# The adds of the modulation sums on VectorE instead of GpSimd, and one modulation block moved to a later stage

## The chip, the cores and the metric

One Trainium2 chip, one of its cores. The metric is the device time of one execution in microseconds, the median of several runs. The kernel computes two transformer blocks in one launch; this text is about a stretch of about 450 us in the first third of it.

## The reference, cut to what matters

Every layer is modulated by rows that come from the conditioning vector `c`: a vector-matrix product with a weight of 1024 x 6144, split into six parts. Here is what the change touches: layer 0's dense feed-forward, and the modulation of layer 1 and of its shared keys and values.

```python
c_act = jax.nn.silu(c)
for layer in range(DEPTH):
    mod = c_act @ w_ada[layer] + b_ada[layer]
    a_shift, a_scale, a_gate, f_shift, f_scale, f_gate = jnp.split(mod, 6, axis=-1)
    if layer == N_A_LAYERS:
        kc, vc, k_slc, v_slc, k_win, v_win = nsa_shared_kv(h, c_act, kv_gain, w_kv_ada, b_kv_ada, ...)
    u = modulate(rmsnorm(h, attn_gain[layer]), a_shift, a_scale)
    ...

def modulate(u, shift, scale):
    return u * (1.0 + scale[:, None, :]) + shift[:, None, :]

def swiglu(u, wg, wu, wd):
    return (jax.nn.silu(u @ wg) * (u @ wu)) @ wd
```

There are 256 tokens, a width of 1024, and a hidden width of 2816 in the dense layer.

## The kernel before, in words

**Stages.** `run` goes through layer 0's attention, its dense feed-forward (`ffn0`, about 190 to 431 us of the trace), layer 1's projections and attention (`layer1`, `layer1_out`, about 431 to 656 us), and then a mixture of experts, a second mixer and a second mixture. Weights come from HBM in chunks of 128 x 2048 f32 (1 MB), all issued in one order on SyncE's queue (SP). The instructions of each engine are put in an order by a scheduler when the program is built; on the chip every engine, and SP with its transfers, takes them strictly in that order.

**The dense stage.** 11 steps, each with three 1 MB chunks: gate (`ffg`), up (`ffu`), down (`ffd`). Products are made exact enough by splitting a weight into a high and a low part: ScalarE copies `raw` to `wh` (L425), VectorE subtracts to get `wl` (L426), and TensorE multiplies three times. `gu` are the gate and up products (48 matmuls each, L454, L455, L457), `ffacc` the down products (24 matmuls a step, L462 to L464), one step behind. Between them ScalarE applies silu (`hid`, L936), VectorE multiplies (L937) and splits the result into `hh` and `hl` (L425, L426). There are four `raw` buffers, three `wh`, three `wl`.

**Modulation blocks.** A block is 1024 x 2048 of a modulation weight, 8 chunks of 1 MB. There are two ways to compute one. `ada_block` (L479 to L493, called by `ada`) streams the chunks through two `adaw` buffers into TensorE: 4 matmuls a chunk, in four column groups of the array (L491), 32 in a block; then `ada_columns` copies the sums (`adaacc`, L502), brings them into columns with 4 small matmuls (L506) and adds the bias (L509). `ada_sums` (L511 to L532) is for stages in which TensorE is busy: ScalarE scales each chunk by its values of `c` (L523), GpSimd adds it to a running sum `adasum` (L525, 7 adds a block), and TensorE sums only over the partitions at the end (4 matmuls, L529). It is a generator: each `next(sums)` in `ffn0` records one chunk. It has four `adaw` buffers and two `adasum` buffers; a buffer's next load waits for the add that reads it.

**Who uses what.** `ffn0` computes four blocks this way: "k" 0 (for the shared keys and values), and "1" 0, 1 and 2 (all of layer 1's). Block "1" 2 holds layer 1's f_scale and f_gate, columns 32 to 47 of `mod1`; they are read by `moe_ahead` in `layer1_out`, behind the attention, and later. `ada("2", 0)` and `ada("2", 1)` are blocks of the second mixer's modulation, computed the direct way in and around layer 1.

Of the kernel before, what the change touches and what calls it, by code (L numbers as in the profile page):

```python
# [14 lines left out]
ALU = mybir.AluOpType  # L15
# [220 lines left out]
class Build:  # L236
# [274 lines left out]
    def ada_sums(self, blocks):  # L511


        nc = self.nc
        for n, b in blocks:
            total = self.act.tile([P, 2048], F32, tag="adasum", name=self.name("adasum"), bufs=2)
            for k in range(8):
                w = total
                if k:
                    pool, bufs = (self.act, 2) if k % 2 else (self.adap, self.ada_bufs)  # L520
                    w = pool.tile([P, 2048], F32, tag="adaw", name=self.name("adaw"), bufs=bufs)
                nc.sync.dma_start(w[:], self.A["ada" + n][b][:, k * 2048:(k + 1) * 2048])
                nc.scalar.activation(w[:], w[:], AF.Identity, scale=self.c_col[:, k:k + 1])  # L523
                if k:
                    nc.gpsimd.tensor_tensor(total[:], total[:], w[:], op=ALU.add)  # L525
                yield
            acc = self.pc([P, 512], name="ada")
            for g in range(4):
                nc.tensor.matmul(acc[32 * g:32 * g + 32, :], self.ones[:, :32], total[:, g * 512:(g + 1) * 512], start=True,  # L529
                                 stop=True, tile_position=(0, 32 * g))  # L530
            s = slice(16 * b, 16 * b + 16)
            self.ada_columns(acc, [({"0": self.mod0, "1": self.mod1, "k": self.modk}[n][:, s], self.sm("b_ada" + n)[:, s])])  # L532
# [371 lines left out]
    def ffn0(self):  # L904
        nc, A = self.nc, self.A
        r = self.rstd(self.h)
        g = self.gain1(self.sm("fg0"), self.mod0[:, 32:40], "fg0")
        u, = self.norm_T(self.h, r, [(g, self.mod0[:, 24:32])])
        acc = [self.pa([P, 2, 512], name="ffacc%d" % m) for m in range(2)]
        pend = []  # L910
        sums = self.ada_sums([("k", 0), ("1", 0), ("1", 1), ("1", 2)])

        def down():
            hid, w, j = pend.pop(0)
            wh, wl = self.split(w)
            for f in range(2):
                for m in range(2):
                    for n in range(2):
                        a = tuple(x[:, f, m * P:(m + 1) * P] for x in hid)
                        b = tuple(x[:, f, n * 512:(n + 1) * 512] for x in (wh, wl))  # L920
                        self.mm3(acc[m][:, n, :], a, b, start=j + f == 0, stop=j + f == 11)

        for j in range(11):
            wgu = [self.load(A[n][j], (8, 256))[0] for n in ("ffg", "ffu")]
            wd = self.load(A["ffd"][j], (2, 1024))[0]
            pg = []
            for i in range(2):
                wh, wl = self.split(wgu[i])
                ps = self.pb([P, 2, 256], name="gu")
                for ff in range(2):  # L930
                    s = slice(ff * P, (ff + 1) * P)
                    self.products_T(ps[:, ff, :], wh[:, :, s], wl[:, :, s], u)
                pg.append(ps)
                next(sums, None)
            hid = self.tl("s2", (2, 256), name="hid")
            nc.scalar.activation(hid, pg[0][:], AF.Silu)  # L936
            nc.vector.tensor_tensor(hid, hid, pg[1][:], op=ALU.mult)  # L937
            hh = self.tl("s2", (2, 256), F32R, name="hh")
            hl = self.tl("s2", (2, 256), F32R, name="hl")
            self.split_to(hh, hl, hid)  # L940
            if j:
                down()
                next(sums, None)
            pend.append(((hh, hl), wd, j))
        self.whole(sums)
        down()
        gate = self.tl("s4", (1024,), name="gate")
        for i in range(2):
            ps = self.pb([P, 4, P])
            for k in range(4):  # L950
                nc.tensor.matmul(ps[:, k, :], self.mod0[:, 40 + 4 * i + k:41 + 4 * i + k].to_broadcast([P, P]), self.ident,
                                 start=True, stop=True)
            nc.scalar.activation(gate[:, i * 512:(i + 1) * 512], ps[:].rearrange("p a b -> p (a b)"), AF.Copy)
        for m in range(2):
            tmp = self.tl("s4", (1024,), name="res")
            nc.vector.tensor_tensor(tmp, acc[m][:].rearrange("p a b -> p (a b)"), gate, op=ALU.mult)
            nc.vector.tensor_tensor(self.h[:, m, :], self.h[:, m, :], tmp, op=ALU.add)
# [137 lines left out]
    def layer1_out(self, qT, br, extra):  # L1095
        A = self.A
        oh = self.tl("s8", (8, 256), F32R, name="oh")
        ol = self.tl("s8", (8, 256), F32R, name="ol")
        self.ada("2", 0)
        with self.banks("att1", 0, 0):  # L1100
            self.attend(qT, br, oh, ol, extra)
        self.ada("2", 1)
        with self.banks("out1", 2, 3):
            gate = self.bcast_row(self.mod1[:, 16:24])
            t = self.moe_ahead(self.sm("rt1"), self.sm("fg1"), self.mod1[:, 32:40], self.mod1[:, 24:32])
            for b in range(2):
                self.residual(self.dense_tok((oh, ol), A["b_out"][b], 512, apart=True), b, gate)
                if b == 0:
                    for m in range(2):
                        self.squares(self.h, self.ss1, m, 0)  # L1110
        return t
# [1226 lines left out]
```

## Time and profile before

| what | us |
|---|---|
| median of 3 runs | 2009.3 (2007.61 to 2012.69) |
| the profiled execution, its own time | 2009.72 |
| its span in the trace | 2007.9 |
| TensorE busy in the span | 1827.2 (91%) |
| VectorE busy | 1013.6 (50%) |
| ScalarE busy | 771.9 (38%) |
| GpSimd busy | 222.0 (11%) |

Between the span and the time of the same execution lie 1.8 us. The busy time of an instruction runs from its start to its end. The granted clock is TensorE's, as a share of 2.4 GHz; it has two levels, and a stretch's value is the mean over them. Idle times in square brackets stand before an instruction and name what ended them.

### The profile page before, as it was taken

How to read it: one execution, taken by the hardware profiler on the slowest of the kernel's cores; microseconds unless marked ns; L12 is line 12 of the kernel's file. 1: busy time of each engine (PE TensorE's matmuls, PEld its weight loads, DVE VectorE, ACT ScalarE, POOL GpSimd, SP SyncE). 2: the span in 40 equal slices, each digit the busy share in tenths (PEclk: the TensorE clock that was granted, in tenths of full speed). 3: DMA queues.
4: the chain of work that ended last, by engine and by line, in shares of the span. 5: the costliest groups of instructions: out<-in, count | busy, mean ns of one | idle time of the engine just before them, and what ended most of it. 6: DMA issues, size and time to landing. Idle time of an engine off the chain costs nothing. (4 is left out here: it accounts for less than half of the span.)

```text
span 2007.9 us, 25685 instructions
## 1 busy us (share of the span) xinstructions
PE 1827.2 (91%) x9658; PEld 1174.9 (59%) x9658; DVE 1013.6 (50%) x1382; ACT 771.9 (38%) x961; POOL 222.0 (11%) x128
## 2 busy tenths in 40 slices
PE   4998799979999799999999999998999699899996
PEld 2656698856756685455555555554554486535452
DVE  3775787775554673344434534444542566524234
ACT  3355556632364463342333333433331453212131
POOL 0100856621000200000000200000000200100000
PEclk8999899989899899999999999999999899899998
DMA  8783577954611699999999999999999425599995
GB/s 338 266 310 147 214 285 299 355 230 155 261 71 51 232 346 384 422 403 376 405 422 402 380 410 377 422 414 402 346 422 421 183 87 208 190 405 354 409 420 214
DMA packets 128947, 624.29 MB, mean 311 GB/s; under 512 B 14512, under 2 KB 14768, under 8 KB 90800
## 3 DMA queue, kind: packets, MB, share of 16 engines
q1 hardware_dynamic: 127552, 619.59, 78.4%
q10 hardware_dynamic: 1264, 2.98, 0.4%
q8 instruction: 79, 1.29, 0.2%
q14 instruction: 52, 0.43, 0.1%
HBM read 621.46 MB, written 1.05 MB: 310 GB/s over the span
## 5 line engine op out<-in xcount | busy, mean ns | idle before, releaser
L426 DVE TENSOR_TENSOR wl<-raw,wh 128x2048 fp32r<-128x2048 f32 (+1 forms) x207 | 526.9, 2554 | 353.5 <-ACT wh L425 308.0
L425 ACT ACTIVATE wh<-raw 128x2048 fp32r<-128x2048 f32 (+1 forms) x207 | 391.4, 1899 | 275.3 <-DMA raw<-in_moe 142.3
L1428 PE MATMUL gu<-raw,xT 128*64 128x512 f32 (+2 forms) x1600 | 353.0, 592 | 9.2 <-DMA raw<-in_moe 9.0
L1428 PEld LDWEIGHTS gu<-raw,xT 128*64 128x64 f32 (+1 forms) x1600 | 102.9, 132 | 206.9 <-issue 162.5
L1428 PE MATMUL down<-raw,hh 128*64 128x512 f32 (+1 forms) x784 | 169.0, 598 | 0.6 <-DMA raw<-in_moe 0.6
L525 POOL TENSOR_TENSOR adasum<-adasum,adaw 128x2048 f32<-128x2048 f32 x28 | 151.5, 5414 | 67.8 <-ACT adaw L523 59.9
L1419 PE MATMUL gu<-wh,xT 128*128 128x512 f32 x368 | 148.6, 404 | 2.1 <-ACT wh L425 2.1
L1420 PE MATMUL gu<-wh,xT 128*128 128x512 f32 x368 | 144.7, 393 | 0.0
L1428 PEld LDWEIGHTS down<-raw,hh 128*64 128x64 f32 (+1 forms) x784 | 49.3, 132 | 90.0 <-issue 78.5
L1422 PE MATMUL gu<-wl,xT 128*128 128x512 f32 x368 | 99.6, 393 | 0.4 <-DVE wl L426 0.4
L1419 PE MATMUL down<-wh,hh 128*128 128x512 f32 (+1 forms) x192 | 82.4, 429 | 17.7 <-ACT wh L425 17.7
L455 PE MATMUL gu<-uh,wl 128*128 128x256 f32 x352 | 88.5, 288 | 6.5 <-DVE wl L426 6.5
L454 PE MATMUL gu<-uh,wh 128*128 128x256 f32 x352 | 88.9, 289 | 3.5 <-ACT uh L627 3.5
L491 PE MATMUL ada<-adaw,act_c 128*32 128x512 f32 x384 | 63.7, 671 | 22.3 <-DVE act_c L475 13.1
L1471 DVE SCALAR_TENSOR_TENSOR hid<-hid,gs,gu 128x512 f32<-128x512 f32 (+1 forms) x46 | 34.0, 739 | 94.2 <-PE gu L1428 47.7
L1420 PE MATMUL down<-wh,hl 128*128 128x512 f32 (+1 forms) x192 | 80.2, 418 | 0.0
L1419 PEld LDWEIGHTS gu<-wh,xT 128*128 128x128 f32 x368 | 69.7, 189 | 17.0 <-ACT wh L425 3.0
L426 DVE TENSOR_TENSOR hl<-hT,hh 128x512 fp32r<-128x512 f32 (+1 forms) x24 | 16.2, 678 | 124.7 <-ACT hh L425 124.7
L1422 PEld LDWEIGHTS gu<-wl,xT 128*128 128x128 f32 x368 | 69.4, 189 | 16.2 <-DVE wl L426 1.3
L425 ACT ACTIVATE hh<-hT 128x512 fp32r<-128x512 f32 (+1 forms) x24 | 14.0, 588 | 167.1 <-PE hT L1386 167.1
L1420 PEld LDWEIGHTS gu<-wh,xT 128*128 128x128 f32 x368 | 69.8, 190 | 13.7
L1469 ACT ACTIVATE hid<-gu 128x512 f32<-128x512 f32 (+1 forms) x46 | 27.3, 593 | 129.5 <-PE gu L1428 114.0
(627 smaller groups left out, 2893.3 us busy)
## 6 DMA issues: line engine op xcount, KB each, us to landing
raw<-in_moe SPq DMA_DIRECT2D x580, 512.0 KB, 9.9
raw<-in_moe SPq DMA_DIRECT2D x142, 1024.0 KB, 11.1
adaw<-in_ada SPq DMA_DIRECT2D x69, 1024.0 KB, 6.9
raw<-in_ffg SPq DMA_DIRECT2D x11, 1024.0 KB, 6.2
raw<-in_ffu SPq DMA_DIRECT2D x11, 1024.0 KB, 5.1
raw<-in_ffd SPq DMA_DIRECT2D x11, 1024.0 KB, 5.1
raw<-in_a_in SPq DMA_DIRECT2D x8, 1024.0 KB, 6.5
adaw<-in_adak SPq DMA_DIRECT2D x7, 1024.0 KB, 7.8
```

Source lines behind the costliest of these rows:

```text
L425: self.nc.scalar.activation(hi, src, AF.Copy)
L426: self.nc.vector.tensor_tensor(lo, src, hi.bitcast(F32), op=ALU.subtract)
L454: nc.tensor.matmul(out, wh[:, k, :], u[0][:, k, :], start=k == 0, stop=False)
L455: nc.tensor.matmul(out, wl[:, k, :], u[0][:, k, :], start=False, stop=False)
L491: nc.tensor.matmul(acc[32 * g:32 * g + 32, :], c[:, k, :], w[:, g * 512:(g + 1) * 512], start=k == 0, stop=k == 7, tile_position=(0, 32 * g))
L525: nc.gpsimd.tensor_tensor(total[:], total[:], w[:], op=ALU.add)
L1419: nc.tensor.matmul(ps, x[0], w(0, 0), start=start, stop=False)
L1420: nc.tensor.matmul(ps, x[1], w(0, 0), start=False, stop=False)
L1422: nc.tensor.matmul(ps, x[0], w(1, 0), start=False, stop=stop)
L1428: nc.tensor.matmul(ps[c], x[0][:, c], w(k // 2, k % 2), start=start, stop=stop, tile_position=(0, n * k))
L1469: nc.scalar.activation(hid[it, i], pg[i, 0][:, :nh], AF.Silu)
L1471: nc.vector.scalar_tensor_tensor(hid[it, i], hid[it, i], gs[e, i], pg[i, 1][:, :nh], op0=ALU.mult, op1=ALU.mult)
```

## The change

The add of a scaled chunk to the running sum (L525) is issued on VectorE instead of GpSimd. `ffn0` computes three blocks instead of four, so that two `next(sums)` a step do where there were three. The fourth block, "1" 2, is computed in `layer1_out` the direct way, between `ada("2", 0)` and the attention.

```diff
@@ ada_sums
                 nc.scalar.activation(w[:], w[:], AF.Identity, scale=self.c_col[:, k:k + 1])
                 if k:
-                    nc.gpsimd.tensor_tensor(total[:], total[:], w[:], op=ALU.add)
+                    nc.vector.tensor_tensor(total[:], total[:], w[:], op=ALU.add)
                 yield
@@ ffn0
-        sums = self.ada_sums([("k", 0), ("1", 0), ("1", 1), ("1", 2)])
+        sums = self.ada_sums([("k", 0), ("1", 0), ("1", 1)])
...
             if j:
                 down()
-                next(sums, None)
             pend.append(((hh, hl), wd, j))
@@ layer1_out
         self.ada("2", 0)
+        self.ada("1", 2)
         with self.banks("att1", 0, 0):
             self.attend(qT, br, oh, ol, extra)
         self.ada("2", 1)
```

What it does to the order of VectorE, where the first step's gate and up products end. Before (numbers in names tell tiles apart; `adaw` and `adasum` are a chunk and the sum):

```order
L633 TENSOR_TENSOR ul_1330<-uT_1359,uh_1329 128x1024
L937 TENSOR_TENSOR hid_1490<-hid_1490,gu_1437 128x512
L426 TENSOR_TENSOR wl_1561<-raw_1499,wh_1560 128x2048
L426 TENSOR_TENSOR hl_1494<-hid_1490,hh_1493 128x512
L426 TENSOR_TENSOR wl_1625<-raw_1375,wh_1624 128x2048
L426 TENSOR_TENSOR wl_1663<-raw_1656,wh_1662 128x2048
L937 TENSOR_TENSOR hid_1617<-hid_1617,gu_1564 128x512
```

The same place on VectorE after the change:

```order
L633 TENSOR_TENSOR ul_1330<-uT_1359,uh_1329 128x1024
L525 TENSOR_TENSOR adasum_1430<-adasum_1430,adaw_1711 128x2048
L525 TENSOR_TENSOR adasum_1430<-adasum_1430,adaw_1768 128x2048
L525 TENSOR_TENSOR adasum_1430<-adasum_1430,adaw_1866 128x2048
L937 TENSOR_TENSOR hid_1490<-hid_1490,gu_1437 128x512
L426 TENSOR_TENSOR wl_1561<-raw_1499,wh_1560 128x2048
L426 TENSOR_TENSOR wl_1625<-raw_1375,wh_1624 128x2048
L426 TENSOR_TENSOR hl_1494<-hid_1490,hh_1493 128x512
L525 TENSOR_TENSOR adasum_1430<-adasum_1430,adaw_1923 128x2048
L426 TENSOR_TENSOR wl_1659<-raw_1652,wh_1658 128x2048
L937 TENSOR_TENSOR hid_1617<-hid_1617,gu_1564 128x512
```

Three adds now stand ahead of the first `hid` and one ahead of the third `wl`; three more stand further ahead, among the norm's instructions, and 14 further down, one or two in a step.

TensorE at the start of layer 1's attention, before (`sc` are scores, `pt` transposes, `o` outputs; `ada` with L491 is a chunk of a block):

```order
L1067 MATMUL pb_3913<-kcbd_3850,qT_3868 128x32 x8
L491 MATMUL ada_4585<-adaw_4616,act_c_3188 32x512
L772 MATMUL sc_3999<-kbd_3499,qT_3868 128x2x128
L774 MATMUL sc_3999<-causr,identr 128x2x128
L772 MATMUL sc_4005<-kbd_3499,qT_3868 128x2x128
L774 MATMUL sc_4005<-causr,identr 128x2x128
L491 MATMUL ada_4585<-adaw_4616,act_c_3188 32x512 x3
L491 MATMUL ada_4585<-adaw_4622,act_c_3188 32x512 x4
L772 MATMUL sc_4027<-kbd_3521,qT_3868 128x2x128
```

And after the change:

```order
L1066 MATMUL pb_3870<-kcbd_3807,qT_3825 128x32 x8
L491 MATMUL ada_3950<-adaw_3987,act_c 32x512 x4
L772 MATMUL sc_4012<-kbd_3456,qT_3825 128x2x128
L774 MATMUL sc_4012<-causr,identr 128x2x128
L772 MATMUL sc_4018<-kbd_3456,qT_3825 128x2x128
L774 MATMUL sc_4018<-causr,identr 128x2x128
L491 MATMUL ada_3950<-adaw_3993,act_c 32x512 x4
L772 MATMUL sc_4040<-kbd_3478,qT_3825 128x2x128
L774 MATMUL sc_4040<-causr,identr 128x2x128
L506 MATMUL ada_3950<-const,adaacc_3999 128x4 x4
```

What stands here before is the end of the second mixer's second block; after the change it is the end of the moved block, and the second mixer's second block is spread over the attention behind it.

SP's transfers at the end of the stage, before (`in_moe` are the experts' first weights):

```order
L403 DMA raw_4765<-in_b_out 128x2048
L489 DMA adaw_4616<-in_ada 128x2048
L489 DMA adaw_4622<-in_ada 128x2048
L489 DMA adaw_4628<-in_ada 128x2048
L1362 DMA raw_4924<-in_moe 128x2048
L1362 DMA raw_4982<-in_moe 128x2048
```

And after the change:

```order
L403 DMA raw_4778<-in_b_out 128x2048
L489 DMA adaw_3987<-in_ada 128x2048
L489 DMA adaw_3993<-in_ada 128x2048
L489 DMA adaw_4599<-in_ada 128x2048
L489 DMA adaw_4605<-in_ada 128x2048
L489 DMA adaw_4611<-in_ada 128x2048
L489 DMA adaw_4617<-in_ada 128x2048
L489 DMA adaw_4623<-in_ada 128x2048
L489 DMA adaw_4629<-in_ada 128x2048
L489 DMA adaw_4635<-in_ada 128x2048
L489 DMA adaw_4641<-in_ada 128x2048
L1362 DMA raw_4937<-in_moe 128x2048
```

Ten chunks of blocks stand ahead of the experts' first weights there, instead of three.

## Rows read from the trace of the kernel before

**Rows 1.** The page's first part: busy time, share and instructions of each engine.

```profile
PE 1827.2 (91%) x9658; PEld 1174.9 (59%) x9658; DVE 1013.6 (50%) x1382; ACT 771.9 (38%) x961; POOL 222.0 (11%) x128
```

**Rows 2.** Dense stage, windows: busy us (instructions) PE, PEld, DVE, ACT, POOL; clock; DMA; GB/s.

```profile
219.60:262.00 42.40, 33.01 (x192) 29.88 (x192) 38.78 (x11) 22.42 (x15) 32.91 (x6) 0.84 0.61 230
262.00:340.00 78.00, 75.78 (x529) 69.28 (x528) 58.60 (x24) 49.00 (x33) 43.36 (x10) 0.98 0.80 312
340.00:422.40 82.40, 78.49 (x523) 69.49 (x522) 67.19 (x26) 47.40 (x33) 54.12 (x10) 0.98 0.75 294
```

**Rows 3.** TensorE's waits, 219 to 423 us: in total, times, longest.

```profile
PE gu L455 <- DVE wl L426: 6.5, 2, 5.6
PE ffacc L463 <- DVE wl L426: 5.7, 3, 3.8
PE ada L506 <- ACT adaacc L502: 2.2, 1, 2.2
```

**Rows 4.** Groups by line and form, 196 to 424 us: busy, mean ns; idle before.

```profile
L525 POOL TENSOR_TENSOR adasum<-adasum,adaw 128x2048 f32<-128x2048 f32 x28 | 151.5, 5414 | 67.8 <-ACT adaw L523 59.9 <-issue 6.8
L426 DVE TENSOR_TENSOR wl<-raw,wh 128x2048 fp32r<-128x2048 f32 x32 | 130.4, 4088 | 32.8 <-ACT wh L425 32.8
...
L523 ACT ACTIVATE adaw<-adaw,act_c 128x2048 f32<-128x2048 f32 x26 | 52.0, 2003 | 14.0 <-DMA adaw<-in_ada 8.3 <-DMA adaw<-in_adak 5.7
...
L937 DVE TENSOR_TENSOR hid<-hid,gu 128x512 f32<-128x512 f32 x11 | 7.5, 678 | 10.2 <-ACT hid L936 7.7 <-PE gu L457 2.5
```

**Rows 5.** VectorE's timeline around the first stall: start, us, instruction, count.

```profile
216.98 0.69 DVE L937 TENSOR_TENSOR hid<-hid,gu 128x512 f32<-128x512 f32 x1 [7.69 <-ACT hid L936]
218.79 6.42 DVE L426 TENSOR_TENSOR wl<-raw,wh 128x2048 fp32r<-128x2048 f32 x1 [1.12 <-ACT wh L425]
225.14 5.08 DVE L426 TENSOR_TENSOR hl<-hid,hh 128x512 fp32r<-128x512 f32 x1
...
244.65 0.69 DVE L426 TENSOR_TENSOR hl<-hid,hh 128x512 fp32r<-128x512 f32 x1 [0.70 <-ACT hh L425]
246.46 2.29 DVE L426 TENSOR_TENSOR wl<-raw,wh 128x2048 fp32r<-128x2048 f32 x1 [1.11 <-ACT wh L425]
```

**Rows 6.** GpSimd's timeline in the same stretch.

```profile
198.13 43.07 POOL L525 TENSOR_TENSOR adasum<-adasum,adaw 128x2048 f32<-128x2048 f32 x8 [6.78 <-issue]
```

**Rows 7.** TensorE's timeline in the dense stage: where groups of products begin.

```profile
219.42 0.28 PE L454 MATMUL gu<-uh,wh 128*128 128x256 f32 x1
...
281.14 0.28 PE L454 MATMUL gu<-uh,wh 128*128 128x256 f32 x1
...
292.54 0.39 PE L462 MATMUL ffacc<-wh,hh 128*128 128x512 f32 x1
...
298.11 0.28 PE L454 MATMUL gu<-uh,wh 128*128 128x256 f32 x1
...
422.40 1.95 PE L951 MATMUL pb<-const,mod 128*128 128x128 f32 x16
```

**Rows 8.** TensorE's timeline in layer 1: chunks of blocks (the trace counts two per matmul).

```profile
440.77 1.92 PE L491 MATMUL ada<-adaw,act_c 128*32 128x512 f32 x16
...
496.52 1.06 PE L506 MATMUL ada<-const,adaacc 128*128 128x8 f32 x8 [0.71 <-ACT adaacc L502]
...
572.97 1.05 PE L491 MATMUL ada<-adaw,act_c 128*32 128x512 f32 x2
```

**Rows 9.** TensorE's waits for chunks and norm, 424 to 628 us.

```profile
PE ada L491 <- DMA adaw<-in_ada: 6.3, 2, 4.0
PE nT L619 <- DVE dr L613: 4.7, 2, 4.0
```

**Rows 10.** Windows of layer 1's attention and behind it, columns as in the windows above.

```profile
553.00:627.00 74.00, 70.32 (x380) 36.90 (x378) 46.80 (x107) 44.29 (x158) 0.00 (x0) 0.98 0.11 44
580.00:640.00 60.00, 56.88 (x330) 34.22 (x329) 31.85 (x60) 31.65 (x100) 0.00 (x0) 1.00 0.00 1
```

**Rows 11.** SP's timeline at the attention's start.

```profile
558.11 0.86 SPq L1362 DMA_DIRECT2D raw<-in_moe  x2
```

## The prediction

> **What bounds the kernel now.** I read the page's busy times first: TensorE is busy for 91% of the span [rows 1], so an edit that takes work off other engines gains only where TensorE waits. The edit touches the dense stage, so next come the windows of that stage [rows 2]: from 262 us on TensorE is busy for 75.8 of 78.0 us and 78.5 of 82.4 us at a clock of 0.98, but in the first 42.4 us it is busy for 33.0 only, at 0.84. The stage is bound by TensorE, with a hole at its start. TensorE's timeline gives its length and its full pace [rows 7]: the products behind the first three groups run from 219.42 to 422.40, which is 202.98 us, and at full pace a pair of gate and up products takes 292.54 - 281.14 = 11.40 us and a step's down products 298.11 - 292.54 = 5.57. In this stretch stand 5.70 (the rest of the first step) + 9 x 11.40 + 11 x 5.57 = 169.6 us of such work. Four blocks end there, each with four sums of L529 (one group, about 1.0, as the groups of rows 8) and four of L506, put at 0.8 together by an estimate below the 1.06 of eight such records [rows 8]: 4 x 1.8 = 7.2. That makes 176.8, and **26.2 us are lost**. TensorE's waits name about half: 6.5 and 5.7 us for `wl` on VectorE, 2.2 for `adaacc` [rows 3]. Of the rest, about 10 are the clock's: (1 - 0.84) x 42.4 = 6.8, and 0.02 x (78.0 + 82.4) = 3.2 [rows 2]. TensorE waits there, and the windows with the waits are those with the lower level in them.
>
> **Why VectorE is late.** At 218.79 one `wl` takes 6.42 us and the `hl` behind it 5.08; at 246.46 and 244.65 the same two forms take 2.29 and 0.69 [rows 5]. Over the stage 32 `wl` take 4.088 on average [rows 4], that is 32 x 1.8 = 57 us more than at 2.29. Beside the slow ones GpSimd adds without a pause, 43.07 us from 198.13 to 241.2 [rows 6]; once this row ends, the instructions are short. `hid`, which reads one operand from PSUM, stays at 0.678 on average all the while [rows 4] and takes 0.69 at 216.98 in the middle of GpSimd's run [rows 5]. So the two engines hold each other up when both read SBUF with two operands. The Trainium skill, SBUF — State Buffer, Who interferes with whom, says that a VectorE instruction with two SBUF inputs and a GpSimd instruction on SBUF exclude each other for the whole instruction, and that one SBUF input doesn't suffer; by the rows of `hl` and `hid` the trace agrees, and the sum goes by those rows.
>
> **Part 1: the adds go to VectorE.** 28 adds leave GpSimd (151.5 us, 5414 ns each [rows 4], nothing else of the stage is done there). 21 come to VectorE. An add there isn't in the trace; the nearest row is `wl`, also two SBUF operands of 128 x 2048, at 2.29 undisturbed [rows 5]; bounds are this and the 4.09 of the disturbed mean. I take 2.29, as GpSimd is then silent. A step of VectorE is 3 x 2.29 (`wl`) + 0.69 (`hl`) + 0.68 (`hid`) + 2 x 2.29 = 12.8 us, against 11.40 + 5.57 = 17.0 of TensorE: 4.1 us to spare, so the adds are covered by products. If the cover is gone (all at 4.09) it is 5 x 4.09 + 1.4 = 21.8, and VectorE bounds; that is a rival below. At the start six adds stand ahead of the first `hid`; the three directly ahead of it need 6.9 us, and VectorE waited 7.69 there [rows 5]. So `hid` may come about where it was, `wl` ends at about 220 instead of 225.2, and the two `wl` behind it, disturbed before, each come some 2 to 4 us sooner. The wait of 5.6 [rows 3] and most of 5.7 go. ScalarE scales 24 chunks instead of 32 (2003 ns each [rows 4]), which gives it time and gives TensorE none.
>
> How much of the 26.2 goes? All of it is the upper bound. I keep 4: the 2.2 for `adaacc` [rows 3], which the change doesn't touch, and about 2 for what is tight at the start. So 22.2 us come back, and one block's end less gives 1.8: **a gain of 24.0**, at most 28.0.
>
> **What is late next.** Two adds a step have to find their chunks scaled: ScalarE waited 14.0 us in the stage for chunks [rows 4], and a faster stage wants more bytes in each us: 5 chunks in 17.0 us are 309 GB/s, against 312 seen in the middle of the stage with all six chunks of a step [rows 2]. So transfers are no new bound.
>
> **Part 2: the block goes to layer 1.** It costs TensorE 32 matmuls in four column groups. Four that lie together cost about 1.0 us (two groups: 1.92), but one alone costs 1.05 as well [rows 8]. Counted in the order, there are 22 such groups from the end of the dense stage to the end of the attention before, and 30 after: +8 x 1.0. The block's L506 adds 1.06 [rows 8]: 9.1. Off goes what falls where TensorE waits anyway: it waits 4.7 us for the norm [rows 9], and the order now has 24 matmuls ahead of that wait's end and around it instead of 16: -2. On comes +1 for chunks that are late: TensorE waited 6.3 us for two of them [rows 9], and the two buffers still set the pace of SP. I take **8.0**. Bounds: the low end fills also the idle time of the attention, 74.00 - 70.32 = 3.7 [rows 10]: 4.3. The high end is 9.1 and two more waits of 4.0 each [rows 9]: 17.
>
> **What SP is moved past.** The first two loads of the experts, issued at 558.11 [rows 11], now stand behind ten chunks, not three. I cost that at nothing: from 580 to 640 the queue is empty, a DMA share of 0.00 [rows 10], because the next weights wait for buffers, and seven chunks need, each a group of matmuls apart, only part of that. If the last chunk is used later than about 640 us, the cover is gone and each further us counts in full.
>
> **The sum.** 2009.72 - 24.0 + 8.0 = **1993.7** against the profiled execution. The median is 0.4 below it; rounded, 1994.
>
> **Rivals.**
> (a) *All of the loss goes and layer 1 hides half of the block*: 2009.7 - 28.0 + 4.3 = 1986.0. For it: the order of the attention has the groups apart, between softmax steps. Against: a group costs its 1.0 wherever TensorE is not waiting, and it is busy for 95% there [rows 10].
> (b) *Half of the stall stays.* The start is tight: six adds go before the first `hid`, a late chunk there shifts `hid` and `wl`, and TensorE stays at the lower level. Gain 24 - 10 = 14, then 2003.7.
> (c) *VectorE becomes the bound*: `wl` stays at 4.09 without GpSimd's help. VectorE was busy for 38.78 + 58.60 + 67.19 = 164.6 us [rows 2] and gets 15 adds behind 219.4 (34.4): 199 of 203. The gain is 4, the time 2013.7. Against it stand the 2.29 and 0.69 right after GpSimd's run [rows 5]. The Trainium skill, Perfetto Trace Analysis, Optimizing Scalar/DVE Operations, has a rule against this change: with VectorE saturated, work may be given to ScalarE or even GpSimd. By that rule the time is (c)'s; the rows say that VectorE is saturated only while GpSimd adds.
> (d) *Slower: VectorE waits in order.* An add that isn't ready holds `wl` behind it. GpSimd waited 59.9 us for scaled chunks [rows 4], nearly all behind the first eight adds, so about 3.0 for each of 20. A wait of w costs 2w - 4.1 in a step, over 7.5 steps with two adds. It eats the net gain of 16 at w = 3.1; at 4.0, TensorE's longest wait for a chunk [rows 9], it is 29 us: 2022.7. Against: GpSimd had nothing else to do and came early, while an add on VectorE stands behind `wl`, and its chunk has time to come; ScalarE's own waits for chunks are 14.0 only.
> That the change doesn't do what it says is no case: the order shows adds and block where the diff puts them.
>
> **How the numbers follow.** The forecast (1990 to 2000) gets 0.60, (a) 0.11, (b) 0.16, (c) 0.05, (d) 0.08. The range must hold 8 in 10: it reaches down to (a)'s 1986, and up past (b)'s 2003.7, with 2 us for a dearer block, to 2006; (c) and (d), 0.13, are left out. A block at its high end (17) with the full gain lies inside, at 2002.7. A measurement of this kernel can tell about 0.3% (6 us) from no change, so faster is below 2003.3. The forecast, (a) and half of (b) are faster: 0.79. Half of (b) and (c) are the same: 0.13. (d) is slower: 0.08.
>
> **What would show it.** Right: `wl` of the dense stage near 2.3 us on average; TensorE's waits for `wl` L426 near zero; the clock in the stage's first 42 us above 0.95; the stage from 219 on about 24 us shorter; then 8 us given back between its end and the end of the attention, as eight more groups of L491. Wrong: waits of VectorE for `adaw` L523 above 2 us each, with TensorE behind them (d); `wl` still at 4 (c); a first `hid` well behind 217 and a low clock behind it (b); a wait of TensorE for the experts' first weights, which would mean that SP's ten chunks were not covered.

## The result, and the profile after

The changed kernel takes 1987.01 us (median of 4 executions, 1976.84 to 1987.57) against 2008.45 of the kernel before in the same set: a ratio of 0.9876, 95% interval [0.9847, 0.9906], so 24.9 us less by that ratio (19 to 31). Set against the 2009.3 that the prediction started from, that is 1984.4 us. The direction was right, and the forecast of 1994 lies above the measured interval; the range's low end of 1986 was 1.6 us too high.

The profiled execution of the changed kernel took 1976.84 us, its span is 1974.8. Its engines, for [rows 1]:

```profile
PE 1814.3 (92%) x9714; PEld 1162.8 (59%) x9714; DVE 977.3 (49%) x1403; ACT 756.2 (38%) x953; POOL 68.6 (3%) x100
```

VectorE got 21 adds and is busy 36 us less than before. GpSimd lost 153 us.

The windows of the dense stage, for [rows 2] (us; busy us and instructions of PE, PEld, DVE, ACT, POOL; granted clock, mean DMA share, GB/s):

```profile
219.60:262.00 42.40, 42.40 (x307) 39.98 (x306) 37.93 (x22) 30.84 (x21) 0.00 (x0) 1.00 0.84 308
262.00:340.00 78.00, 78.00 (x549) 72.07 (x548) 55.02 (x32) 47.74 (x33) 0.00 (x0) 1.00 0.86 322
340.00:396.50 56.50, 56.50 (x383) 50.16 (x382) 25.06 (x18) 21.22 (x17) 0.00 (x0) 1.00 0.53 179
```

TensorE is busy in every microsecond from 219.6 to the stage's end, at the full clock. The list of its waits from 219 us to the end of the stage, where [rows 3] stood, is empty. The groups by form, for [rows 4] (busy us, mean ns; idle before):

```profile
L426 DVE TENSOR_TENSOR wl<-raw,wh 128x2048 fp32r<-128x2048 f32 x32 | 73.2, 2290 | 46.6 <-ACT wh L425 46.3
L525 DVE TENSOR_TENSOR adasum<-adasum,adaw 128x2048 f32<-128x2048 f32 x21 | 48.0, 2286 | 1.2 <-ACT adaw L523 0.9
L523 ACT ACTIVATE adaw<-adaw,act_c 128x2048 f32<-128x2048 f32 x19 | 37.8, 1998 | 1.6 <-DMA adaw<-in_adak 1.6
```

`wl` went from 4088 to 2290 ns, an add costs 2286 ns instead of 5414 on GpSimd, and VectorE waits only 0.9 us for scaled chunks. VectorE's timeline at the start, for [rows 5]:

```profile
217.65 0.69 DVE L937 TENSOR_TENSOR hid<-hid,gu 128x512 f32<-128x512 f32 x1 [1.58 <-PE gu L457]
218.26 4.49 DVE L426 TENSOR_TENSOR wl<-raw,wh 128x2048 fp32r<-128x2048 f32 x2
222.66 0.68 DVE L426 TENSOR_TENSOR hl<-hid,hh 128x512 fp32r<-128x512 f32 x1
```

The first `hid` is 0.7 us later than before, but two `wl` and `hl` are done at 223.3, where before one `wl` was done at 225.2 and `hl` at 230.2.

To compare kernels I cut each profile in three: the **stage** (from the first product of L454 to the row product of L951, which is L950 after the change), **layer 1** (from there to the start of the last output product of its attention, L810) and the **rest** (to the span's end). The two last cuts of the changed kernel, by source line (first and last start in us):

```profile
L950 PE MATMUL pb<-const,mod x16: 273/275/275, 396.5 to 398.2; 128*128 128x128 f32 x16
L810 PE MATMUL o<-pts,v x96: 379/379/431, 530.9 to 599.4; 128*64 128x256 f32 x96
```

and of the kernel before, whose stage ends at 422.40 [rows 7]:

```profile
L454 PE MATMUL gu<-uh,wh x352: 274/282/561, 196.6 to 403.0; 128*128 128x256 f32 x176
L810 PE MATMUL o<-pts,v x96: 379/379/431, 563.0 to 627.4; 128*64 128x256 f32 x96
```

All runs, with the pieces of their profiles (in us; the kernel before as it stood with them has medians of 2008.7 to 2009.2):

| run | median | ratio to before | stage | layer 1 | rest |
|---|---|---|---|---|---|
| before | 2009.3 | | 225.8 | 205.0 | 1380.5 |
| before, second profile (b4) | 2010.96, one | | 228.3 | 203.4 | 1381.1 |
| changed | 1987.01 | 0.9876 [0.9847, 0.9906] | 199.6 | 202.9 | 1375.4 |
| changed again (a1) | 1986.89 | 0.9882 [0.9855, 0.9909] | 199.7 | 202.9 | 1377.3 |
| changed, third profile (b3) | 1974.51, one | | 198.9 | 202.8 | 1375.6 |
| changed, fourth profile (c2) | 1979.3, one | | 199.0 | 202.7 | 1376.9 |
| four blocks, adds on VectorE (a2) | 1974.92 | 0.9823 [0.9797, 0.9850] | 202.0 | 195.8 | 1377.7 |
| three blocks, adds on GpSimd (a3) | 2003.3 | 0.9961 [0.9943, 0.9980] | 220.0 | 206.8 | 1380.1 |
| changed, without the moved block (a4) | 2151.59 | 1.0703 [1.0673, 1.0734] | 201.5 | 198.8 | 1555.5 |
| first block's adds on VectorE (b1) | 1985.55 | 0.9881 [0.9857, 0.9905] | 210.1 | 198.4 | 1375.8 |
| five blocks, adds on VectorE (b2) | 1985.62 | 0.9881 [0.9865, 0.9897] | 218.5 | 192.1 | 1370.3 |
| four adds on GpSimd, 24 on VectorE (c1) | 1985.52 | 0.9892 [0.9859, 0.9924] | 208.6 | 205.0 | 1374.4 |

Stage and layer 1 of one kernel repeat well: the changed kernel's layer 1 is 202.7 to 202.9 in four profiles, and the two profiles of the kernel before differ by 2.5 us in the stage and 1.6 in layer 1. So differences of 3 us and more between kernels are read from here. What stands out at once: the stage gave 26 us (24 were forecast), but **layer 1 did not give 8 back; it became 2 us shorter** although it got a block more.

### The profile page after: what moved, and what is told of

Same layout as the page of the kernel before. It is cut to its first block, busy times and chain, and to the rows that moved or that the text cites. A ratio compares the mean times of both kernels' runs of the same rounds, so it can differ in the third digit from the quotient of the medians.

```text
span 1974.8 us, 25753 instructions
## 1 busy us (share of the span) xinstructions
PE 1814.3 (92%) x9714; PEld 1162.8 (59%) x9714; DVE 977.3 (49%) x1403; ACT 756.2 (38%) x953; POOL 68.6 (3%) x100
## 5 line engine op out<-in xcount | busy, mean ns | idle before, releaser
L426 DVE TENSOR_TENSOR wl<-raw,wh 128x2048 fp32r<-128x2048 f32 (+1 forms) x207 | 470.1, 2277 | 362.3 <-ACT wh L425 318.3
L491 PE MATMUL ada<-adaw,act_c 128*32 128x512 f32 x448 | 71.6, 665 | 23.8 <-DVE act_c L475 12.3
L454 PE MATMUL gu<-uh,wh 128*128 128x256 f32 x352 | 87.2, 285 | 1.9 <-ACT uh L627 1.9
L445 PE MATMUL pa<-wh,uh 128*128 128x512 f32 (+2 forms) x176 | 68.7, 397 | 7.2 <-DVE uT L631 7.2
```

The costliest lines, as they stand in the source:

```text
L426: self.nc.vector.tensor_tensor(lo, src, hi.bitcast(F32), op=ALU.subtract)
L445: nc.tensor.matmul(out, a[0], b[0], start=start and i == 0, stop=False)
L454: nc.tensor.matmul(out, wh[:, k, :], u[0][:, k, :], start=k == 0, stop=False)
L491: nc.tensor.matmul(acc[32 * g:32 * g + 32, :], c[:, k, :], w[:, g * 512:(g + 1) * 512], start=k == 0, stop=k == 7, tile_position=(0, 32 * g))
```

## The experiments

### The two parts apart

Each run has its expectation ahead of it; the letters (T, R, C and so on) are the theories named there. a1 is the changed kernel once more.

> The changed kernel once more, for its spread and a second profile. Theory T (GpSimd's adds held VectorE up; the moved block costs TensorE 8 us in layer 1): the dense stage from its first product to its end again near 200 us, layer 1 from the dense stage's end to the end of the attention near 203 us in every profile. Rival R (the block costs layer 1 next to nothing): the same total, as this run alone doesn't tell them apart. Rival C (part of what the first profile shows is the clock in places that the change doesn't touch): the total of this profile differs by several us, and the difference lies outside the dense stage.

It took 1986.89, with the same stage and layer 1. The profiled executions of the changed kernel (1976.84, 1979.49, 1974.51, 1979.3) are all shorter than most of its other executions, near 1987; the kernel before and the kernel of a2 show no such gap. More on that at the end.

a2 is part 1 alone, all four blocks in the stage:

```diff
-                    nc.gpsimd.tensor_tensor(total[:], total[:], w[:], op=ALU.add)
+                    nc.vector.tensor_tensor(total[:], total[:], w[:], op=ALU.add)
```

> Part 1 alone: adds on VectorE, all four blocks in the dense stage, nothing in layer 1. T: the stage ends 1.8 us later than in the changed kernel (the fourth block's sums), layer 1 is 8 us shorter: 1987 - 6 = 1981. R: 1987 + 2 = 1989. Rival V (VectorE or the transfers fill up with 28 adds): waits for wl or ffacc come back and the stage is 10 us or more longer, 1995 or more.

It took **1974.92**, faster than T's 1981 and faster than the changed kernel: the interval of its ratio, [0.9797, 0.9850], ends below that of a1, [0.9855, 0.9909]. Its stage is full to the end, although it holds four blocks (windows, columns as above):

```profile
219.60:262.00 42.40, 42.40 (x312) 39.32 (x312) 38.35 (x22) 31.18 (x22) 0.00 (x0) 1.00 0.83 316
340.00:400.00 60.00, 60.00 (x411) 53.60 (x410) 41.30 (x27) 33.96 (x24) 0.00 (x0) 1.00 0.84 323
```

The fourth block costs the stage 202.0 - 199.6 = 2.4 us (1.8 was taken). In layer 1 the same block costs 202.9 - 195.8 = 7.1 us (8.0 was taken). So both prices of the block were about right, and V, that 28 adds fill VectorE, is out. R, that the block costs layer 1 next to nothing, is out too. What wasn't forecast is that layer 1, with the very same work as before, takes 195.8 instead of 205.0 or 203.4.

a3 is part 2 alone, three blocks with the adds left on GpSimd:

```diff
-        sums = self.ada_sums([("k", 0), ("1", 0), ("1", 1), ("1", 2)])
+        sums = self.ada_sums([("k", 0), ("1", 0), ("1", 1)])
...
+        self.ada("1", 2)
```

> Part 2 alone: adds on GpSimd, three blocks there, the fourth in layer 1. T: the first eight adds still come back to back, so the stall at the start stays; the stage gains the block's end (1.8) and some 4 us, layer 1 loses 8: 2009 + 2 = 2011, wl near 3.7 us on average. Rival L (fewer blocks in the stage is what helped, not the engine): the stage is 20 us or more shorter, 1995 or less.

It took 2003.3, ratio 0.9961 [0.9943, 0.9980], and not T's 2011. The stage shrank by 5.8 us, to 220.0, which is T's 1.8 + 4; the stall stands where it stood (TensorE's waits from 219 us on, then the groups of the stage):

```profile
PE ffacc L463 <- DVE wl L426: 8.2, 3, 4.5
PE gu L455 <- DVE wl L426: 6.4, 2, 5.5
```

```profile
L426 DVE TENSOR_TENSOR wl<-raw,wh 128x2048 fp32r<-128x2048 f32 x32 | 116.4, 3651 | 44.9 <-ACT wh L425 44.9
L525 POOL TENSOR_TENSOR adasum<-adasum,adaw 128x2048 f32<-128x2048 f32 x21 | 108.0, 5143 | 64.4 <-ACT adaw L523 57.1 <-issue 6.8
L426 DVE TENSOR_TENSOR hl<-hid,hh 128x512 fp32r<-128x512 f32 x11 | 25.1, 2285 | 0.7 <-ACT hh L425 0.7
```

`wl` is at 3651 ns (3.7 was expected) and `hl` at 2285 ns instead of 684. So it is the engine that helps, not the smaller number of blocks: L is out. But here too layer 1 with a block more is only 206.8, 2 to 3 above before, where T said 8; with the stage as T had it, this is where T's total was too high.

a4 leaves the moved block out: block "1" 2 is not computed, and its columns of `mod1` are zero.

```diff
-        self.ada("1", 2)
+        self.nc.vector.memset(self.mod1[:, 32:48], 0.0)
```

> The changed kernel without the moved block: block 1, 2 is not computed, its columns of the modulation are set to zero. T: layer 1 is 8 us shorter, 1979. R: 1985 to 1987.

Its total says nothing here: the mixtures behind layer 1 get other values, and the rest takes 1555.5 us. Layer 1 stands ahead of that. It takes 198.8, which looks like 4.1 for the block, against 7.1 by a2. But the clocks differ. Layer 1 as one window, of a4, a3 and the changed kernel:

```profile
398.60:597.40 198.80, 181.16 (x997) 117.41 (x997) 118.47 (x213) 88.84 (x215) 11.29 (x24) 0.93 0.40 152
416.70:623.50 206.80, 191.83 (x1071) 121.25 (x1069) 119.70 (x216) 89.78 (x216) 11.29 (x24) 0.93 0.51 186
396.50:599.40 202.90, 188.08 (x1071) 118.33 (x1070) 119.64 (x216) 89.72 (x216) 11.29 (x24) 0.95 0.51 190
```

a4 and a3 have the same order and the same 0.93, one without the block and one with it: it costs 206.8 - 198.8 = 8.0. a2 and the changed kernel are both at 0.95: 7.1. So at nearly equal clock the block's price is 7.1 to 8.0, and the 4.1 is not a price of the block alone.

### What costs in the stage, and how much VectorE bears

b1 puts only the seven adds of the first block on VectorE; 21 stay on GpSimd:

```diff
-                    nc.gpsimd.tensor_tensor(total[:], total[:], w[:], op=ALU.add)
+                    e = nc.vector if n == "k" else nc.gpsimd
+                    e.tensor_tensor(total[:], total[:], w[:], op=ALU.add)
```

> The kernel before with the seven adds of the first block alone on VectorE, the 21 of the other three blocks on GpSimd, four blocks in the stage. T (it is the run of adds at the start, while TensorE's products wait for VectorE, that costs; later stretched wl are covered by products): the stage from its first product to its end takes 203 to 210 us instead of 225.8, although wl stays well above 3 us on average; the total is near 1988. Rival E (every add on GpSimd costs alike): 7 of 28 adds give a quarter of the 24, the stage takes 219 or more, the total is 2003 or more.

The stage takes 210.1 (203 to 210 was T's, 219 or more E's), the total is 1985.55 (near 1988 was T's). The groups of the stage:

```profile
L426 DVE TENSOR_TENSOR wl<-raw,wh 128x2048 fp32r<-128x2048 f32 x33 | 118.2, 3595 | 27.5 <-ACT wh L425 27.5
L526 DVE TENSOR_TENSOR adasum<-adasum,adaw 128x2048 f32<-128x2048 f32 x7 | 16.0, 2287 | 1.1 <-ACT adaw L523 0.9
```

`wl` is still at 3595 ns (4088 with all adds on GpSimd), and yet 15.7 of the 23.8 us that a2's stage gained are there. So a stretched `wl` later in the stage is mostly covered by products: from 262 to 340 us GpSimd is busy for 57.5 us and TensorE for 77.5 of 78.0. It is the run of adds at the start [rows 6] that TensorE pays for most; the other 21 adds cost the remaining 8.1 us. E is out.

b2 goes the other way, with a fifth block (the second mixer's second) in the stage, and a fourth `next(sums)` in a step (cut: the set-up of the second mixer moves ahead of the stage, and its chunks are scaled by its own values):

```diff
-        sums = self.ada_sums([("k", 0), ("1", 0), ("1", 1), ("1", 2)])
+        sums = self.ada_sums([("k", 0), ("1", 0), ("1", 1), ("1", 2), ("2", 1)])
...
                 down()
                 next(sums, None)
+                next(sums, None)
...
-        self.ada("2", 1)
```

> All adds on VectorE and five blocks in the dense stage: the second mixer's second block, which the kernel before computes in layer 1's attention, is summed there too. T (a summed block costs the stage 1.8 us, a block in layer 1 costs 7 to 8): the stage takes 204 us, layer 1 188, the total is 1975 - 6 = 1969. Rival D (33 + 40 transfers of 1 MB in 200 us are 383 GB/s, more than the stage has shown): TensorE waits in the stage for weights, the total is 1975 or more.

Layer 1 falls to 192.1, but the stage grows to 218.5, and the total of 1985.62 is worse than a2's. T, which had the stage at 204 and the total at 1969, is out. Of what D expected, the total came true and the reason didn't: TensorE doesn't wait for weights, and where the transfers are fastest, it is busy nearly all the time (a window of the stage as above):

```profile
262.00:340.00 78.00, 77.60 (x555) 70.77 (x554) 58.22 (x35) 53.86 (x37) 0.00 (x0) 1.00 0.96 385
```

TensorE's waits in the stage, and VectorE's:

```profile
PE gu L455 <- DVE wl L426: 6.5, 3, 2.3
PE ada L506 <- ACT adaacc L502: 1.1, 2, 0.7
PE gu L454 <- ACT wh L425: 0.7, 1, 0.7
```

```profile
DVE wl L426 <- ACT wh L425: 16.2, 11, 2.7
DVE adasum L525 <- ACT adaw L523: 12.9, 7, 3.4
```

and one of these waits in VectorE's timeline:

```profile
376.01 2.28 DVE L525 TENSOR_TENSOR adasum<-adasum,adaw 128x2048 f32<-128x2048 f32 x1
381.58 2.29 DVE L525 TENSOR_TENSOR adasum<-adasum,adaw 128x2048 f32<-128x2048 f32 x1 [3.29 <-ACT adaw L523]
```

VectorE's waits for `wh` say little: in a2 they are longer (37.5 us) and TensorE waits for nothing. The waits for scaled chunks are what a2 hasn't got. I read this as the prediction's rival (d): with four adds a step VectorE's work is 12.8 + 2 x 2.29 = 17.4 us against TensorE's 17.0, an add that waits in order has no slack to wait in, and `wl` behind it is late. VectorE is not full, though: from 340 to 406 us, where TensorE loses its time, it is busy for 50.8 of 66.0 us. So the load alone doesn't explain it; no run takes it and the waiting in order apart. With three adds a step (15.1, a2) no add waited from 219 us on.

### Why layer 1 got shorter

The order of TensorE's instructions in layer 1 is the same in the changed kernel, a2, a3, a4 and b1 around the norm, and it differs from the kernel before. The rows there before (`nT` are the norm's transposes):

```
L491 MATMUL ada_3936<-adaw_3937,act_c_3188 32x512 x4
L491 MATMUL ada_3936<-adaw_3943,act_c_3188 32x512 x4
L619 MATMUL nT_3222<-dr_3215,h 128x128
```

In the others three chunks stand ahead of the norm instead of two, and three right behind it instead of two and a quarter; so in a2 the last matmul of the second mixer's two blocks starts at 529.3, ahead of the attention's outputs, and in the kernel before at 575.1, in the midst of them. The prediction saw this and put it at -2. Among the kernels with four blocks in the stage, the first block's adds go with it: with them on VectorE the new order comes out (a2, b1), with them on GpSimd the old one. a3, with three blocks, has the new order although all its adds are on GpSimd. That makes a test, with four blocks and only the first four adds on GpSimd. c1:

```diff
-                    nc.gpsimd.tensor_tensor(total[:], total[:], w[:], op=ALU.add)
+                    (nc.gpsimd if n == "k" and k <= 4 else nc.vector).tensor_tensor(total[:], total[:], w[:], op=ALU.add)
```

> Four blocks in the dense stage, the first four adds of the first block on GpSimd, the other 24 on VectorE. With these four on GpSimd the instructions of layer 1 stand in the order of the kernel before (two chunks of a block ahead of the norm, not three, and one chunk more in the attention). Theory O (that order costs layer 1 what four blocks on VectorE gained there): the stage takes 203 to 212 us, but layer 1 takes 202 to 205, as before; total 1983 or more. Rival N (layer 1 gains because the stage ends otherwise, with GpSimd silent and the clock up): layer 1 takes 196 to 198, total 1976 to 1980.

The old order comes out. `wl` is at its own 2290 ns, the stage takes 208.6, and layer 1 takes **205.0**, the value of before: O holds, N is out. The cuts, and the stretch as one window (of before, a2, c1 and b1; the same columns as above):

```profile
L951 PE MATMUL pb<-const,mod x16: 273/275/275, 404.1 to 405.8; 128*128 128x128 f32 x16
L810 PE MATMUL o<-pts,v x96: 379/379/431, 544.7 to 609.1; 128*64 128x256 f32 x96
```

```profile
422.40:628.00 205.60, 185.84 (x1001) 119.70 (x1000) 118.50 (x213) 89.73 (x216) 10.87 (x24) 0.93 0.41 154
```

```profile
400.10:596.50 196.40, 178.62 (x1001) 115.46 (x1000) 118.52 (x213) 89.09 (x216) 11.33 (x24) 0.95 0.41 153
```

```profile
404.10:609.10 205.00, 185.45 (x997) 118.50 (x998) 118.40 (x213) 89.47 (x215) 10.84 (x24) 0.93 0.41 152
```

```profile
409.70:609.00 199.30, 182.30 (x1004) 118.68 (x1002) 118.57 (x213) 89.32 (x216) 11.31 (x24) 0.93 0.41 153
```

The instructions are the same thousand. From before to a2 TensorE is busy 7.2 us less and idle 2.0 less (205.60 - 185.84 = 19.8, 196.40 - 178.62 = 17.8). Of the idle time, the wait for the norm falls from 4.7 [rows 9] to this:

```profile
PE nT L619 <- DVE ss L598: 1.7, 1, 1.7
```

The clock can be told apart by the stretches of layer 1 at its lower level (1.2 GHz), as windows of their own, summed. In before there are five, in a2 four:

```profile
sum 30.60, PE 26.89 PEld 18.75 DVE 15.13 ACT 8.51 POOL 3.26; mean PE 5.38 PEld 3.75 DVE 3.03 ACT 1.70 POOL 0.65
sum 20.40, PE 17.97 PEld 9.93 DVE 10.98 ACT 5.56 POOL 3.26; mean PE 4.49 PEld 2.48 DVE 2.74 ACT 1.39 POOL 0.82
```

So TensorE is busy at the lower level for 26.9 us in before and for 18.0 in a2; the same sums are 25.4 in b4 and 26.8 in c1, 25.2 in b1, 24.5 in a4, 18.1 in the changed kernel and 26.0 in a3. Half of such time is lost, by the ratio of the levels (an estimate), so the clock gave a2 4.5 us. Some of the busy time is in the chunks of the blocks, 1.7 us less, part of which can be the clock's too (before, then a2):

```profile
L491 PE MATMUL ada<-adaw,act_c 128*32 128x512 f32 x128 | 25.1, 668 | 6.8 <-DMA adaw<-in_ada 6.3 <-PE ada L506 0.5
```

```profile
L491 PE MATMUL ada<-adaw,act_c 128*32 128x512 f32 x128 | 23.4, 697 | 9.3 <-DMA adaw<-in_ada 7.9 <-issue 1.3
```

Without the time lost at the lower level, layer 1 takes 190.7 to 191.6 us in the old order (before twice, c1) and 185.8 to 186.8 in the new one (a2, b1, a4): **the order is worth 4 to 6 us, and the clock up to 4.5 more**. The clock's part doesn't follow from the order alone: against before it is 4.5 in a2, and with the same order only 0.9 in b1 and 1.2 in a4. What decides it these runs don't tell.

### Two more profiles

> The kernel before again, for a second profile. T: stage 225.8. If layer 1 from the stage's end to the end of the attention again takes 205.0, the 9 us that four blocks on VectorE gained there are an effect of part 1; if it takes 197 to 202, they were the clock of one execution (C).

Layer 1 takes 203.4, the stage 228.3 for T's 225.8. Layer 1 of the kernel before is long in both profiles, so C is out for this term: it is no accident of one execution.

> The changed kernel a third time, for another profile. T: stage 199.6, layer 1 to the end of the attention 202.9 as in the two profiles, and a total between 1977 and 1989. C: what parts totals of 1977 and 1988 lies behind the attention, in the clock of stretches that the change doesn't touch.

> The changed kernel again, for a fourth profile: the three before it have spans near 1973 to 1978, while most of its timed executions took 1987. T: stage 199 to 200, layer 1 202.9. If the total is near 1987, the profile shows where the 10 us lie; C says behind the attention.

Stage and layer 1 came as T had them in both, within 0.7 us; the total of b3, 1974.51, is below T's 1977 to 1989. Neither profile was one of the executions near 1987, so they don't show where those lose their 10 us.

## Why the prediction was wrong, step by step

**The diagnosis held.** VectorE was late because GpSimd added beside it, TensorE waited, and the clock fell with the waits. `wl` came to 2290 ns (2.29 taken), the add to 2286 (2.29 taken, bounds 2.29 and 4.09), the waits for `wl` to zero, the clock of the first 42 us from 0.84 to 1.00 (above 0.95 was named). By the Trainium skill, SBUF — State Buffer, Who interferes with whom, an instruction with two SBUF inputs suffers and one with a single SBUF input doesn't: the rows agree again, `hl` at 2285 in a3 against 684 to 685 where GpSimd is silent, and `hid` at 686 in the changed kernel against 678 before. The other rule weighed, of the Trainium skill, Perfetto Trace Analysis, Optimizing Scalar/DVE Operations, has VectorE saturated as its case, and that case isn't here: in the stage VectorE was busy for 154.3 of 202.0 us with all 28 adds (a2). The prediction also left out the sentence that follows the rule there, that the two engines share an SBUF read port, so that moving work between them might not help; the 4088 and 2290 ns of `wl` agree with that.

**The stage: -24.0 taken, -26.2 measured** (225.8 to 199.6; 28.7 against the second profile of before). Of the 4 us that I kept as lost, none stayed: the window from 219.6 on has no idle time. The work at full pace was a little undercounted: 175.0 for three blocks, by the prediction's sum, against the 176.9 from 219.6 to 396.5. The tight start was read rightly (a first `hid` at 217.65, 0.7 us later than before, and the first `wl` done at 220.5 by halving its row of two, "about 220"). One block's end was 2.4 for 1.8.

**Layer 1: +8.0 taken, -2.1 measured.** This is the step that failed, and not by the block's own price: at nearly equal clock that is 7.1 or 8.0, where 8.0 was taken, though with the -2 in it. TensorE's time in L491 rose from 23.4 (a2) to 33.6 us, 10.2 for 8 groups:

```profile
L491 PE MATMUL ada<-adaw,act_c 128*32 128x512 f32 x192 | 33.6, 667 | 9.4 <-DMA adaw<-in_ada 8.0 <-issue 1.3
```

Two things were wrong. The first is the term "Off goes what falls where TensorE waits anyway: ... -2": it took the new order around the norm for a discount on the block, but the order shortens all of layer 1, with the block or without it, by 4.7 us from before to a2 (4 to 6 over the runs) apart from the clock. The second is a term that the sum put at nothing, without a reason: TensorE's clock in layer 1. TensorE is busy at the lower level for 18.1 us in the changed kernel and for 26.9 in before, which is 4.4 us by the estimate above. Together, with a2's 4.7 and 4.5: +7.1 - 4.7 - 4.5 = -2.1. I had counted the groups in both orders and priced only the norm's wait; what stood behind it in layer 1 I took as it was in the trace of before. The low end of the range had the same flaw: 4.3 as the least that layer 1 could cost presumed that nothing else in layer 1 moves.

Part of it is luck: a3 runs the same layer 1 in the same order as the changed kernel, is busy for 26.0 us at the lower level instead of 18.1, and takes 206.8. Half of the difference is 3.9 us, all that parts it from the changed kernel's 202.9. So most of what the clock gave doesn't come from the order, and where it comes from stays open.

**The transfers: cost nothing, as taken.** The experts' first loads are issued at 577.78 instead of 558.11 [rows 11], behind ten chunks on SP:

```profile
515.30 62.42 SPq L489 DMA_DIRECT2D adaw<-in_ada  x10
577.78 55.29 SPq L1362 DMA_DIRECT2D raw<-in_moe  x10
```

and TensorE's waits from the attention's end into the mixture name no transfer, neither before nor after.

**The rivals.** (a) was nearest to the result, with the full loss gone, though not for its reason: layer 1 hid no half of the block, which cost 7.1 to 8.0. (b) is what c1 shows in small: at the start an add on VectorE waits for GpSimd's sum, and TensorE for the `wl` behind it (VectorE's timeline, then TensorE's waits in c1's stage):

```profile
217.13 4.69 DVE L525 TENSOR_TENSOR adasum<-adasum,adaw 128x2048 f32<-128x2048 f32 x2 [9.17 <-POOL adasum L525]
```

```profile
PE gu L455 <- DVE wl L426: 6.3, 1, 6.3
```

(c) is refuted by the 2290 ns. (d) did not come with the two adds a step of this change, nor with a2's three; in b2, with four, VectorE waits as (d) has it.

**The sum.** In the profiles: -26.2 (stage), -2.1 (layer 1), -5.1 (rest), +0.3 (ahead of the stage) = -33.1 us of span. By the medians it is 21.4, and 16.0 was forecast. That the forecast missed the median by only 7 us is luck: most executions of the changed kernel lose some 10 us that the profiles don't show. The rest is the part that nobody touched; it takes 1380.5 and 1381.1 in the two profiles of before and 1375.4 to 1377.3 in the four of the changed kernel, and I don't explain these 3 to 6 us.

**What stays open.** Most executions of the changed kernel take 1987 us, its four profiled ones 1974.5 to 1979.5. So its stage and layer 1 are shown by the profiles, but some 10 us of its usual time lie where no profile of mine saw them. With them a2 is 12 us faster by the medians; by the pieces of the profiles it should be 4.7 (2.4 more in the stage, 7.1 less in layer 1).

**The better version** is part 1 alone (a2): 1974.92 us, 1.8% below the kernel before. The fourth block costs TensorE 2.4 us summed in the stage, and 7.1 to 8.0 in layer 1. With three adds a step this held; with four (b2) it did not.

## What to carry to other kernels

An engine that is off the critical path can set the pace through another engine's instructions: compare the same form's duration beside and away from the suspect (2.29 and 6.42 us here) before you call an engine slow or busy. Price a moved piece of work against the stage as it will be ordered, not as it stood: the new order was worth 4 to 6 us here, against 7.1 to 8.0 for the piece. Compare two kernels' stages at equal clock: the same block looked like 4.1 us where the clocks differed. When one change does two things, time each alone; here part 1 alone was faster than both parts together.

## What the runs showed of the hardware that was not expected

Most of the instructions that GpSimd slowed cost TensorE little: with 21 adds still on GpSimd and `wl` at 3595 ns, 15.7 of 23.8 us came back (b1).

About a thousand identical matmuls of layer 1 took 203.4 to 205.0 us in one order (before twice, c1) and 195.8 to 198.8 in another (a2, b1, a4). Of that, TensorE's clock is up to 4.5 us (an estimate from its busy time at the lower level), and it differed between runs of the same order: 18.0 us at that level in a2, 25.2 in b1, 24.5 in a4.
